# A hybrid decoder trunk on one core: mixer work moved from GpSimd to VectorE, score tiles of one PSUM bank, new spacings in the written order

## The chip, the cores and the metric

One core of a Trainium2 chip runs the whole program, one launch. The metric is the device time of that launch in microseconds (us); less is better. Everything is float32. Matrix products run on TensorE (PE), elementwise work on VectorE (DVE), ScalarE (ACT) and GpSimd (POOL); SyncE (SP) issues the loads of weights. TensorE writes its products to PSUM, 8 banks of 512 float32 per partition, and GpSimd does not touch PSUM anywhere in this program.

## The reference

Two layers, each of three sub-layers on a residual stream x of 512 positions by 1024 features; each sub-layer starts with an RMS norm that is scaled and shifted by values from the vector c, and ends with a gate from c:

```
for l in range(2):
    x += 0.5 * g1 * swiglu_1(mod(norm(x)))          # 1024 -> 2 x 2816 -> 1024
    x += g2 * W_out [ HGRN2 | sparse attention | Mamba-2 ] (mod(norm(x)) @ W_in)
    x += 0.5 * g3 * swiglu_2(mod(norm(x)))
return rms_norm(x)
```

The middle sub-layer, the mixer, holds three independent mixers side by side. HGRN2 (4 heads of 64) is a gated linear recurrence, done in chunks with exact decays. The sparse attention (4 heads of 64, one key and value head) first scores all earlier keys with 8 small index heads, `sum_h w[t,h] relu(q_idx[t,h] . k_idx[s])`, keeps the 128 best for each query, and runs softmax attention over these. Mamba-2 (8 heads of 64, state 128) has a convolution of 4 taps, SiLU, a chunked scan with decays `exp(a_cs[t] - a_cs[s])`, and a gated norm.

## The kernel before, in words

**Products in three parts.** Each float32 operand is split in a high part and the rest (`hi`, `lo`), and each product is three matmuls that accumulate: hi by hi, lo by hi, hi by lo (`mm3`, L342 to L346). A weight is loaded (`wraw`), copied to `whi` on ScalarE (L315), and `wlo = wraw - whi` is made by VectorE, or by GpSimd for the chunks listed in `GF` (L316). There are three buffers of `whi` and `wlo`.

**Feed-forward.** `ffn` runs 22 hidden blocks of 128 and then the product back, in two halves. The next sub-layer's first product starts on the unnormed x while the sum of squares is still on its way; `lead` (L267 on) does that, and folds the shift in by a small product `pb` of a weight that was multiplied with the shift: on GpSimd over 1024 columns (L272), then reduced on VectorE (L276).

**The mixer.** `mixer_woven` holds one dense source and four chains, each a generator that issues instructions and yields how long it wants to wait. `weave` (L327 on) keeps a clock of planned time (`tick`), takes the first whose time has come, and so writes down TensorE's order; TensorE then runs exactly in that order, whatever the real times are. `mark` and `need` tie chains together by planned times; `need_pair` and `hold_pair` book one of two PSUM pairs. The other engines' orders follow the order in which the instructions are traced, their priority, and a list scheduler; `keep_in_program_order` fixes single instructions.

- Dense: the projections (L524, L542 to L544), in the order of `DORD`: forget gates and queries of HGRN2, index keys and queries, attention queries, HGRN2 values, the 8 convolution blocks (`d_conv`: three VectorE steps each at L655, SiLU at L657), then z and g, then the first part of the output projection (`first_out`).
- `topk` scores the index heads (ipl, L706; relu on ScalarE L712, scaled at L719 and summed on GpSimd at L720); `select` takes the 128 best per query in 16 rounds of VectorE's max-of-8 and replace (L732, L735) for each of three blocks.
- `hgrn`: cumulated log decays bf; then seven levels of block sizes 64 down to 1. A level makes differences of bf (L771, L772, VectorE), their exponential (L773, ScalarE), products with k and q (L774, L775, GpSimd), 16 small matmuls into a PSUM pair (lsc, L749), and a predicated copy into the score tile asc (L795). Then four steps over the state (hps, L831 to L863).
- `attends`: scores (apl, L885), maximum and exponential (L895, L898), transposes (apt, L905) and values (apo, L916).
- `ssd`: dt by a series (L933 to L954), cumulated decays (pacs, L957), per block row transposes (prow, L977), decays mt (L1007, L1008), outputs (py) and states (pst).

At the end `project` does the second part of the output projection (po) and adds it to x (L215).

PSUM before: two banks for the dense products (tag mm), two for small ones (sm), and two pairs of two banks (pair). A pair is one tile, and it is free again when its last reader has finished.

Of the kernel before, what the change touches and what calls it, by code (L numbers as in the profile page):

```python
# [18 lines left out]
P = 128  # L19
D = 1024  # L20
S = 512
# [18 lines left out]
LEVLAT = 9.0  # L40
ATTLAT = 10.0
IDXLAT = 3.6
HP = 500
ORD = 'atsh'
DORD = 'hiqvc'
HOLD = 3.5
RES = 4
MTLAT = 8.0
# [6 lines left out]
GF = (6, 7, 8, 9, 10, 11, 12, 13, 14, 15, 16, 17)  # L55
# [9 lines left out]
def body(nc, tc, A):  # L65
    ctx = ExitStack()
    with ctx:
# [199 lines left out]
        def lead(l, i, ws, ps):  # L267
            ts = []
            with tc.high_priority(WAHEAD):
                for wh, wl, raw in ws:  # L270
                    r4 = raw.rearrange("p (a b m) -> p a b m", a=4, b=2)
                    GP.tensor_tensor(r4, r4,  # L272
                                     mod[l][:, i * 6:i * 6 + 4, 1::2][:, :, :, None].to_broadcast([P, 4, 2, P]),
                                     op=OP.mult)
                    r = act("A", "shw", shape=(P, P))
                    V.tensor_reduce(r, raw.rearrange("p (q m) -> p m q", q=NF), axis=AX.X, op=OP.add)  # L276
                    ts.append(r)
# [72 lines left out]
        def begin(pre):  # L350
            with tc.high_priority(0):
# [15 lines left out]
                for step in SEQ:  # L367
# [11 lines left out]
                    else:  # L379
                        j = len(W)  # L380
                        if j < 2:
                            pre[j] = mm("pg"), sm("pu")
                        else:
                            t = pair("pgu")
                            pre[j] = t[:, 0], t[:, 1]
# [108 lines left out]
        def mixer(l, nxt):  # L494
            iqp = pair("pq")
            iqp = [iqp[:, c] for c in range(2)]
# [4 lines left out]
        def mixer_woven(l, nxt, iqp, hh, hl, sb, rb):  # L501
# [123 lines left out]
            def d_index():  # L625
# [5 lines left out]
                mark("ik", 18.0)  # L631
# [14 lines left out]

            def d_conv():
                for f in range(NF):
# [8 lines left out]
                    ACT.activation(t, t, AF.Silu)  # L657
                    xbc.append(t)
                mark("xbc", 6.0)

            def dense():
                hold_pair(16.0)
                for c in DORD:
                    yield from dict(h=d_forget, i=d_index, q=d_query, v=d_value, c=d_conv)[c]()
# [6 lines left out]
                mark("sz", 2.0)  # L671
                sg[:] = [act("C", "sg", shape=(P, 2, 256)) for _ in range(2)]
                yield from tm_group("winG", 256, 4, lambda bp, pp: ACT.activation(sg[bp], pp, AF.Silu))
                mark("sg", 2.0)
                yield from first_out()
# [4 lines left out]
            def topk():  # L680
                yield need("ik")
                for kr in kr_:
                    if kT:
                        yield 3.0
# [11 lines left out]
                for j in range(1, NB):  # L696
# [3 lines left out]
                    for h in range(0, IH, hs):  # L700
# [3 lines left out]
                        for i in range(hs):  # L704
                            ph = slice(i % 2 * 64, i % 2 * 64 + 64)
                            PE.matmul(pl[:, i % 2, i // 2 * n:i // 2 * n + n], iqr[(h + i) // 2][ph, blk(j)],  # L706
# [3 lines left out]
                        for u in range(2):  # L710
                            rl = act("A", "irl")
                            ACT.activation(rl[:, :hs // 2 * n], pl[:, u, :hs // 2 * n], AF.Relu)  # L712
# [31 lines left out]
            def head_pair(name, kx, qx):  # L744
                ps = pair(name)
                for b in range(NB):
                    for u in range(2):
                        ph = slice(u * 64, u * 64 + 64)
                        PE.matmul(ps[:, u, blk(b)], kx[ph, blk(b)], qx[ph, blk(b)], start=True, stop=True)  # L749
# [4 lines left out]
            def hgrn():  # L754
# [11 lines left out]
                def level(m):  # L766
# [6 lines left out]
                    ACT.activation(e, e, AF.Exp)  # L773
                    GP.tensor_tensor(ee[:, :, 0], ee[:, :, 0], v4(k, m)[:, :, 0], op=OP.mult)  # L774
                    GP.tensor_tensor(ee[:, :, 1], ee[:, :, 1], v4(q, m)[:, :, 1], op=OP.mult)  # L775
                    return e

                Asc = [act("B", "asc", shape=(P, 2, S)) for _ in range(2)]
                cur = level(LEVELS[0])
                for f in range(2):  # L780
                    yield need_pair()
                    ps = head_pair("ldg", k[:, f], q[:, f])
                    V.tensor_tensor(b8(Asc[f]), b8(ps), ident[:, None, :].to_broadcast([P, 2 * NB, P]), op=OP.mult)
                ready = clk[0] + 9.0
                for li, m in enumerate(LEVELS):
                    xl = cur
                    for f in range(2):
                        yield need_pair(ready + 2.0 * f)
                        ps = head_pair("lsc", xl[:, f], xl[:, f])
                        if m == 64:  # L790
                            ACT.activation(b8(Asc[f])[:m, :, m:], b8(ps)[:m, :, m:], AF.Copy)
                        else:
                            w = lambda t: t.rearrange("p f (g u m) -> p f g u m", u=2, m=m)[:, :, :, 1]
                            mk = masks[:, li].rearrange("p (g m) -> p g m", m=m)
                            V.copy_predicated(w(Asc[f]), mk[:, None].to_broadcast([P, 2, S // (2 * m), m]), w(ps))  # L795
# [13 lines left out]
                for f in range(2):  # L809
                    for b in range(NB):  # L810
                        PE.transpose(pkd[:, f, blk(b)], k[:, f, blk(b)], ident)
                with tc.high_priority(HP):
                    ACT.activation(kd.rearrange("p f b t -> p (f b t)"), flat(pkd), AF.Copy)
# [9 lines left out]
                for b in range(NB):  # L823
                    yield need_pair(last)
                    last = clk[0] + 7.0
                    hps = pair("hps")
                    po = hps[:, 0, :2 * P].rearrange("p (f c) -> p f c", f=2)
                    vb = vv[b // 2][:, b % 2]
                    if b < NB - 1:
                        for f in range(2):  # L830
                            PE.matmul(hps[:, 1, blk(f)], kd[:, f, b], vb[:, blk(f)], start=True, stop=True)  # L831
# [9 lines left out]
                    hold_pair(4.0)  # L841
                    if b < NB - 1:
                        for f in range(2):
                            pk = hps[:, 1, blk(f)]
                            sn = hst[b % 2][f]
                            for u in range(2):
                                ph = slice(u * 64, u * 64 + 64)
# [406 lines left out]
```

## Time and profile before

| what | value |
|---|---|
| median of 3 runs | 2166.75 us (2165.58 to 2168.28) |
| the profiled execution | 2167.88 us, its span 2166.1 us |
| TensorE matmul busy | 2070.3 us, 96% |
| VectorE busy | 1300.9 us, 60% |
| ScalarE busy | 825.1 us, 38% |
| GpSimd busy | 324.0 us, 15% |
| DMA | 262.5 MB, 121 GB/s on the mean |

The mixer of layer 0 stands at about 415 to 732 us of the span, that of layer 1 at about 1475 to 1792. A share over the span mixes these with feed-forward stretches in which TensorE hardly pauses. The granted clock is a mean of the two levels, 1.2 and 2.4 GHz, as a share of the higher. A row's "waited for" names what released the engine by the profile; for a tile of PSUM that can be the reader that emptied the buffer.

### The profile page before, as it was taken

The numbers are of one execution on the slowest core, as the hardware profiler recorded it, in microseconds if no ns is written. First come the engines' busy times: TensorE is split into PE (matmuls) and PEld (weight loads), VectorE is DVE, ScalarE is ACT, GpSimd is POOL, SyncE is SP. The second block draws the span as 40 slices with busy tenths as digits, with TensorE's granted clock in tenths as the row PEclk, the third lists the DMA queues.
The fourth block names the chain that finished last, engine by engine and source line by source line (L and its number), as shares of the span: only waits on it lengthen the run. The fifth ranks groups of instructions, "written<-read, shape, count | busy, mean of one in ns | idle before, by whom it ended". The sixth has DMA issues, their size and how long they took to land.

```text
span 2166.1 us, 26665 instructions
## 1 busy us (share of the span) xinstructions
PE 2070.3 (96%) x10201; PEld 1711.5 (79%) x10201; DVE 1300.9 (60%) x2338; ACT 825.1 (38%) x1249; POOL 324.0 (15%) x232
## 2 busy tenths in 40 slices
PE   4999999998999999999999999999988999999998
PEld 3888888786787788888878888887767887888886
DVE  7766564688976766433476743357799576333333
ACT  4422223445664432222342222235456644222233
POOL 4000000347401200000010000023662020000001
PEclk9999999999999999999999999999999999999999
DMA  8566562332110356432346753232212123333322
GB/s 304 188 199 235 178 208 85 108 100 57 49 52 30 119 194 237 149 97 86 98 136 214 274 153 97 83 95 91 79 49 59 37 61 98 91 88 113 97 80 77
DMA packets 103536, 262.50 MB, mean 121 GB/s; under 512 B 12272, under 2 KB 14960, under 8 KB 103408
## 3 DMA queue, kind: packets, MB, share of 16 engines
q1 hardware_dynamic: 100016, 256.60, 37.2%
q10 hardware_dynamic: 3392, 4.20, 0.7%
q8 instruction: 80, 1.31, 0.3%
q14 instruction: 48, 0.39, 0.1%
HBM read 255.50 MB, written 2.10 MB: 119 GB/s over the span
## 4 chain that ended last, share of the span: by engine, by line
PE 74%; DVE 14%; ACT 4%; POOL 3%; issue 3%; DMA 2%; ACTq 1%; SPq 0%; POOLq 0%; DVEq 0%
PE pg L344 7%; PE pu L346 7%; PE pg L345 7%; PE pu L344 7%; PE pu L345 7%; PE pg L346 7%; PE pd L345 7%; PE pd L344 7%; PE pd L346 7%; DVE xbc L655 2%; DVE iacc L735 2%; DVE m L732 1%; DVE wlo L316 1%; ACT whi L315 1%; PE po L345 1%
## 5 line engine op out<-in xcount | busy, mean ns | idle before, releaser
L315 ACT ACTIVATE whi<-wraw 128x1024 fp32r<-128x1024 f32 (+1 forms) x374 | 357.2, 957 | 978.0 <-issue 363.4
L316 DVE TENSOR_TENSOR wlo<-wraw,whi 128x1024 fp32r<-128x1024 f32 (+2 forms) x350 | 388.6, 1111 | 371.5 <-ACT whi L315 370.1
L346 PE MATMUL pd<-ahi,wlo 128*128 128x512 f32 (+1 forms) x715 | 275.9, 386 | 0.0
L345 PE MATMUL pd<-alo,whi 128*128 128x512 f32 (+1 forms) x715 | 275.9, 386 | 0.0
L344 PE MATMUL pd<-ahi,whi 128*128 128x512 f32 (+1 forms) x715 | 275.6, 386 | 0.0
L212 POOL TENSOR_TENSOR sq<-sq 128x512 f32<-128x512 f32 x36 | 48.7, 1353 | 1409.3 <-ACT sq L208 1409.1
L346 PE MATMUL pu<-hhi,wlo 128*128 128x512 f32 x656 | 255.7, 390 | 1.6 <-DVE wlo L316 1.6
L344 PE MATMUL pg<-hhi,whi 128*128 128x512 f32 x656 | 255.9, 390 | 0.0
L344 PE MATMUL pu<-hhi,whi 128*128 128x512 f32 x656 | 255.8, 390 | 0.0
L345 PE MATMUL pg<-hlo,whi 128*128 128x512 f32 x656 | 255.7, 390 | 0.0
L345 PE MATMUL pu<-hlo,whi 128*128 128x512 f32 x656 | 255.4, 389 | 0.0
L346 PE MATMUL pg<-hhi,wlo 128*128 128x512 f32 x656 | 255.4, 389 | 0.0
L173 DVE SCALAR_TENSOR_TENSOR adaw<-adaw,crow 128x512 f32<-128x512 f32 x288 | 192.6, 708 | 5.1 <-DMA adaw<-wada 4.7
L440 DVE TENSOR_TENSOR a<-a,pu 128x512 f32<-128x512 f32 x84 | 57.7, 687 | 202.7 <-PE pu L346 202.4
L345 PEld LDWEIGHTS pd<-alo,whi 128*128 128x128 f32 x715 | 134.3, 188 | 27.1
L344 PEld LDWEIGHTS pd<-ahi,whi 128*128 128x128 f32 x715 | 134.3, 188 | 27.1
L346 PEld LDWEIGHTS pd<-ahi,wlo 128*128 128x128 f32 x715 | 134.3, 188 | 26.9
L346 PEld LDWEIGHTS pu<-hhi,wlo 128*128 128x128 f32 x656 | 123.1, 188 | 28.3 <-DVE wlo L316 2.9
L345 PEld LDWEIGHTS pg<-hlo,whi 128*128 128x128 f32 x656 | 123.1, 188 | 26.7 <-DVE hlo L304 1.0
L344 PEld LDWEIGHTS pg<-hhi,whi 128*128 128x128 f32 x656 | 123.1, 188 | 26.6 <-ACT hhi L299 1.3
L344 PEld LDWEIGHTS pu<-hhi,whi 128*128 128x128 f32 x656 | 123.2, 188 | 26.3 <-ACT whi L315 0.8
L345 PEld LDWEIGHTS pu<-hlo,whi 128*128 128x128 f32 x656 | 123.2, 188 | 25.5
(321 smaller groups left out, 3472.0 us busy)
## 6 DMA issues: line engine op xcount, KB each, us to landing
wraw<-wgu SPq DMA_DIRECT2D x176, 512.0 KB, 3.6
adaw<-wada SPq DMA_DIRECT2D x288, 256.0 KB, 5.0
wraw<-wdn SPq DMA_DIRECT2D x64, 384.0 KB, 3.1
wraw<-wdn SPq DMA_DIRECT2D x64, 320.0 KB, 2.9
wraw<-winF SPq DMA_DIRECT2D x36, 512.0 KB, 3.7
wraw<-woutB SPq DMA_DIRECT2D x16, 384.0 KB, 3.0
wraw<-winC SPq DMA_DIRECT2D x8, 512.0 KB, 3.6
rope<-rraw ACTq DMA_DIRECT2D x48, 64.0 KB, 2.6
```

The source lines that it names most:

```text
L173: V.scalar_tensor_tensor(raw, raw, 1.0, crow[:, h], op0=OP.mult, op1=OP.mult, accum_out=part[:, c, h:h + 1])
L212: (eng if f < NF - 1 else V).tensor_add(ssq_t["t"][:, h], ssq_t["t"][:, h], sq[:, h])
L315: ACT.activation(hi, raw, AF.Copy)
L316: (eng or V).tensor_sub(lo, raw, hi.bitcast(F32))
L344: PE.matmul(ps, wh, xh, start=first, stop=False)
L345: PE.matmul(ps, wh, xl, start=False, stop=False)
L346: PE.matmul(ps, wl, xh, start=False, stop=last)
L440: V.tensor_mul(a, a, pu)
L655: V.scalar_tensor_tensor(t[:, s_:], raw[:, :S - s_], cw(3 - s_), t[:, s_:], op0=OP.mult, op1=OP.add)
L732: first = V.max(m8, acc[:, :n])
L735: V.match_replace(acc[:, :n], m8, acc[:, :n], GONE)
```

## The change

- GpSimd's share of the weight splits falls from 12 chunks per mixer to 3 (`GF`); the products of the levels (`LVE`) and, for block 1, the index sums (`IDXV`) go to VectorE; the lead's shift sums become eight VectorE instructions on 128 columns per weight (`LDG`).
- PSUM: no pairs any more. The tag sm has six banks, and `pair` returns two of them. Readers that took a pair in one instruction take each bank by itself (the predicated copies, the diagonal products, kd). The second part of the output projection uses these banks too. The planner still books two pairs.
- The level exponential is traced after the second score product of the level before and is fixed in order; so is the first exponential of each attention group, now after a yield, and the SiLU of each convolution block, one block later.
- Mamba-2's dt series waits for HGRN2's first state (`DTAT`) and has half the steps; half of the decay differences go from ScalarE to VectorE.
- Planned latencies change, the priority of some small instructions is raised, the chains are taken up in another order. The sizes in `SLOTS` and the tile `lev` are as before in the diff.

```diff
-LEVLAT = 9.0
-ATTLAT = 10.0
-IDXLAT = 3.6
+LEVLAT = 6.0
+ATTLAT = 6.5
+IDXLAT = 5.0
-ORD = 'atsh'
-DORD = 'hiqvc'
-HOLD = 3.5
+ORD = 'thas'
+DORD = 'hiqvcCG'
+HOLD = 2.5
+EXLAT = 2.5
+PTLAT = 4.5
+STLAT = 10.0
+DTAT = 'st'
+IDXV = (1,)
+LVE = 'VV'
+LDG = 0
-MTLAT = 8.0
+MTLAT = 12.0
-GF = (6, 7, 8, 9, 10, 11, 12, 13, 14, 15, 16, 17)
+GF = (10, 11, 12)
...
-            return pq.tile(list(shape), F32, name=name, tag="sm", bufs=2)
+            return pq.tile(list(shape), F32, name=name, tag="sm", bufs=6)
         def pair(name):
-            return pq.tile([P, 2, S], F32, name=name, tag="pair", bufs=2)
+            return [sm(name) for _ in range(2)]
...
+                        t = act("A", "shw", shape=(P, P))
+                        V.tensor_scalar(t, raw[:, blk(0)], shift_of(l, i, 0), None, op0=OP.mult)
+                        for q in range(1, NF):
+                            V.scalar_tensor_tensor(t, raw[:, blk(q)], shift_of(l, i, q), t, op0=OP.mult, op1=OP.add)
+                        ts.append(t)
...
+            def silu(f):
+                tc.keep_in_program_order(ACT.activation(xbc[f], xbc[f], AF.Silu))
...
+                                elif j in IDXV:
+                                    V.scalar_tensor_tensor(acc[:, :n], r, w, acc[:, :n], op0=OP.mult, op1=OP.add)
...
-                    ACT.activation(e, e, AF.Exp)
-                    GP.tensor_tensor(ee[:, :, 0], ee[:, :, 0], v4(k, m)[:, :, 0], op=OP.mult)
-                    GP.tensor_tensor(ee[:, :, 1], ee[:, :, 1], v4(q, m)[:, :, 1], op=OP.mult)
                     return e
+                def level_exp(e, m):
+                    ee = v4(e, m)
+                    tc.keep_in_program_order(ACT.activation(e, e, AF.Exp))
+                    g0, g1 = [GP if c == "P" else V for c in LVE]
+                    g0.tensor_tensor(ee[:, :, 0], ee[:, :, 0], v4(k, m)[:, :, 0], op=OP.mult)
+                    g1.tensor_tensor(ee[:, :, 1], ee[:, :, 1], v4(q, m)[:, :, 1], op=OP.mult)
...
-                        if f == 0 and li + 1 < len(LEVELS):
-                            cur = level(LEVELS[li + 1])
-                            nready = clk[0] + LEVLAT
+                        if li + 1 < len(LEVELS):
+                            if f == 0:
+                                cur = level(LEVELS[li + 1])
+                            else:
+                                level_exp(cur, LEVELS[li + 1])
+                                nready = clk[0] + LEVLAT
...
-                    last = clk[0] + 7.0
+                    last = clk[0] + STLAT
...
+                        yield EXLAT + 0.8 * hs
+                            e = ACT.activation(pe, pe, AF.Exp, scale=0.125, bias=mxs[i], accum_out=rsum[:, h:h + 1])
+                            if i == 0:
+                                tc.keep_in_program_order(e)
...
-                yield need("idx1")
+                yield need(DTAT)
...
-                for c in (15, 13, 11, 9, 7, 5, 3, 1):
-                    V.tensor_mul(dt, dt, u3)
-                    V.tensor_scalar(dt, dt, 1.0 / c, None, op0=OP.add)
-                V.tensor_mul(dt, dt, u2)
+                for c in (17, 15, 13, 11, 9, 7, 5, 3):
+                    V.scalar_tensor_tensor(fl(dt), fl(dt), 1.0 / c, fl(u3), op0=OP.add, op1=OP.mult)
+                V.scalar_tensor_tensor(fl(dt), fl(dt), 1.0, fl(u2), op0=OP.add, op1=OP.mult)
...
+                            if g:
+                                V.tensor_scalar(mt[:, r], pr[g][:, blk(r)], acs[:, b, h:h + 1], 0.0,
+                                                op0=OP.subtract, op1=OP.min)
...
-            for _ in project(KO, mm, lambda f: (*weights(A["woutB"][l, f], 768), 0), nxt, True):
+            po = halves("po")
+            for _ in project(KO, lambda _: next(po), lambda f: (*weights(A["woutB"][l, f], 768), 0), nxt, True):
```

## Rows read from the trace of the kernel before

**Rows 1.** The page's part 1: busy us, share of the span, instructions.

```profile
PE 2070.3 (96%) x10201; PEld 1711.5 (79%) x10201; DVE 1300.9 (60%) x2338; ACT 825.1 (38%) x1249; POOL 324.0 (15%) x232
```

**Rows 2.** Windows: busy us (instructions) of PE, PEld, DVE, ACT, POOL; clock; DMA.

```profile
415.00:732.00 317.00, 293.88 (x1818) 245.07 (x1817) 246.59 (x470) 174.91 (x310) 116.79 (x82) 0.95 0.21 60
732.00:1475.00 743.00, 739.78 (x3273) 609.00 (x3271) 402.22 (x689) 231.02 (x301) 34.95 (x22) 1.00 0.46 147
1475.00:1792.00 317.00, 290.35 (x1819) 242.56 (x1819) 249.23 (x470) 173.32 (x310) 116.66 (x83) 0.96 0.21 62
```

**Rows 3.** Windows inside layer 0's mixer.

```profile
500.00:640.00 140.00, 125.48 (x777) 104.28 (x776) 126.26 (x293) 83.50 (x148) 56.93 (x41) 0.91 0.17 50
510.00:520.00 10.00, 5.99 (x25) 4.70 (x24) 9.62 (x16) 0.46 (x1) 6.78 (x5) 0.66 0.19 52
```

**Rows 4.** TensorE's waits, layer 0's mixer: us in total, times, longest.

```profile
PE ipl L706 <- DVE asc L795: 5.9, 2, 4.0
PE lsc L749 <- ACT irl L712: 3.9, 4, 1.5
PE pf L345 <- DVE hlo L304: 3.8, 2, 2.4
PE prow L977 <- ACT dec L965: 3.2, 1, 3.2
PE hps L831 <- ACT yhg L856: 1.5, 1, 1.5
PE po L345 <- DVE yhl L1103: 1.2, 2, 0.9
```

**Rows 5.** TensorE in order of time: start, us, instruction [idle before].

```profile
514.22 1.65 PE L706 MATMUL ipl<-kT,rope 64*128 64x384 f32 x4 [4.01 <-DVE asc L795]
```

**Rows 6.** VectorE in order of time, layer 0, then 746.89 of the next lead.

```profile
508.26 1.45 DVE L946 TENSOR_TENSOR dt<-dt,spw 128x32 f32<-128x32 f32 x1
...
513.47 0.69 DVE L795 COPY_PREDICATED asc<-masks,lsc 128x512 f32<-128x512 uint8 x1
...
516.85 0.19 DVE L946 TENSOR_TENSOR dt<-dt,spw 128x32 f32<-128x32 f32 x1
...
746.89 1.22 DVE L316 TENSOR_TENSOR wlo<-wraw,whi 128x1024 fp32r<-128x1024 f32 x1
```

**Rows 7.** VectorE by line and shape, 415 to 732: busy us, mean ns.

```profile
L316 DVE TENSOR_TENSOR wlo<-wraw,whi 128x1024 fp32r<-128x1024 f32 x16 | 22.1, 1389 | 4.2 <-ACT whi L315 4.2
...
L795 DVE COPY_PREDICATED asc<-masks,lsc 128x512 f32<-128x512 uint8 x12 | 10.9, 910 | 0.4 <-PE lsc L749 0.4
...
L655 DVE SCALAR_TENSOR_TENSOR xbc<-xraw,vec,xbc 128x510 f32<-128x510 f32 x8 | 7.8, 970 | 0.1
...
L946 DVE TENSOR_TENSOR dt<-dt,spw 128x32 f32<-128x32 f32 x8 | 5.6, 702 | 0.2
...
L771 DVE TENSOR_TENSOR lev<-bf 128x512 f32<-128x512 f32 x7 | 4.8, 681 | 0.0
```

**Rows 8.** VectorE by line and shape, 498 to 600.

```profile
L947 DVE TENSOR_SCALAR dt<-dt 128x32 f32<-128x32 f32 x8 | 5.4, 680 | 0.2
...
L863 DVE TENSOR_TENSOR yhg<-yhg,hss 128x256 f32<-128x256 f32 x4 | 1.7, 420 | 0.2 <-POOL hss L861 0.2
...
L895 DVE CUSTOM_DVE_ANT_0 pexp<-apl,cst 128x128 f32<-128x128 f32 x4 | 0.9, 282 | 0.0
```

**Rows 9.** GpSimd by line and shape, 415 to 732.

```profile
L316 POOL TENSOR_TENSOR wlo<-wraw,whi 128x1024 fp32r<-128x1024 f32 x11 | 27.0, 2456 | 33.3 <-ACT whi L315 33.3
L775 POOL TENSOR_TENSOR lev<-lev,hq 128x512 f32<-128x512 f32 x7 | 11.5, 1637 | 0.0
...
L774 POOL TENSOR_TENSOR lev<-lev,kf 128x512 f32<-128x512 f32 x7 | 10.4, 1483 | 2.1 <-ACT lev L773 2.1
...
L720 POOL TENSOR_TENSOR iacc<-iacc,irl 128x256 f32<-128x256 f32 x7 | 5.8, 833 | 0.4
```

**Rows 10.** ScalarE by line and shape, 415 to 732: idle before.

```profile
L773 ACT ACTIVATE lev<-lev 128x1024 f32<-128x1024 f32 x7 | 7.4, 1058 | 7.4 <-DVE lev L772 5.8 <-DVE lnv L579 1.5
```

More of the change, by code (lines that the diff above doesn't have):

```diff
@@ L268, in lead @@
             ts = []
[L269 to L277, printed above, removed]
+            if LDG:
+                with tc.high_priority(WAHEAD):
+                    for wh, wl, raw in ws:
+                        r4 = raw.rearrange("p (a b m) -> p a b m", a=4, b=2)
+                        GP.tensor_tensor(r4, r4,
+                                         mod[l][:, i * 6:i * 6 + 4, 1::2][:, :, :, None].to_broadcast([P, 4, 2, P]),
+                                         op=OP.mult)
+                        r = act("A", "shw", shape=(P, P))
+                        V.tensor_reduce(r, raw.rearrange("p (q m) -> p m q", q=NF), axis=AX.X, op=OP.add)
+                        ts.append(r)
+            else:
+                with tc.high_priority(WAHEAD):
+                    for wh, wl, raw in ws:
+                        t = act("A", "shw", shape=(P, P))
[3 more added lines that the diff above has]
+                        ts.append(t)
             pb = sm("pb", (P, 2))
@@ L656, in d_conv, with d_z @@
                                                op0=OP.mult, op1=OP.add)
-                    ACT.activation(t, t, AF.Silu)
                     xbc.append(t)
[L659 to L664, printed above, removed]
+                    if f:
+                        silu(f - 1)
+                yield
+                yield
+                yield
+                silu(NF - 1)
+                mark("xbc", 3.0)
+            def d_z():
                 sz[:] = [act("C", "sz") for _ in range(NB)]
@@ L674, in dense @@
                 mark("sg", 2.0)
+            def dense():
+                hold_pair(16.0)
+                for c in DORD:
+                    yield from dict(h=d_forget, i=d_index, q=d_query, v=d_value, c=d_conv, C=d_z, G=d_g)[c]()
                 yield from first_out()
@@ L748, in head_pair @@
                         ph = slice(u * 64, u * 64 + 64)
-                        PE.matmul(ps[:, u, blk(b)], kx[ph, blk(b)], qx[ph, blk(b)], start=True, stop=True)
+                        PE.matmul(ps[u][:, blk(b)], kx[ph, blk(b)], qx[ph, blk(b)], start=True, stop=True)
                 tick(1.15)
@@ L782, in hgrn @@
                     ps = head_pair("ldg", k[:, f], q[:, f])
-                    V.tensor_tensor(b8(Asc[f]), b8(ps), ident[:, None, :].to_broadcast([P, 2 * NB, P]), op=OP.mult)
-                ready = clk[0] + 9.0
+                    for par in range(2):
+                        V.tensor_tensor(b3(Asc[f][:, par]), b3(ps[par]), ident[:, None, :].to_broadcast([P, NB, P]),
+                                        op=OP.mult)
+                level_exp(cur, LEVELS[0])
+                ready = clk[0] + 6.0
                 for li, m in enumerate(LEVELS):
@@ L810, in hgrn @@
                     for b in range(NB):
-                        PE.transpose(pkd[:, f, blk(b)], k[:, f, blk(b)], ident)
+                        PE.transpose(pkd[f][:, blk(b)], k[:, f, blk(b)], ident)
                 with tc.high_priority(HP):
-                    ACT.activation(kd.rearrange("p f b t -> p (f b t)"), flat(pkd), AF.Copy)
+                    for f in range(2):
+                        ACT.activation(kd[:, f], b3(pkd[f]), AF.Copy)
                 mark("kd", 0.0)
@@ L830, in hgrn @@
                         for f in range(2):
-                            PE.matmul(hps[:, 1, blk(f)], kd[:, f, b], vb[:, blk(f)], start=True, stop=True)
+                            PE.matmul(hps[1][:, blk(f)], kd[:, f, b], vb[:, blk(f)], start=True, stop=True)
                     for f in range(2):
@@ L963, in ssd @@
                 dec = sp.tile([P, 3, NB, SH], F32, name="dec", bufs=1)
-                V.tensor_copy(fl(acs), pa[:, 0])
-                ACT.activation(dec.rearrange("p i b h -> p i (b h)"), pa, AF.Exp)
+                with tc.high_priority(HP):
+                    V.tensor_copy(fl(acs), pa[:, 0])
+                    ACT.activation(dec.rearrange("p i b h -> p i (b h)"), pa, AF.Exp)
                 dsd = act("A", "dsd", shape=(P, 4, P))
@@ L969, in ssd @@
                 sss = sp.tile([P, NB, 2], F32, name="sss")
+                yield 3.0
                 def decays(b):
@@ L1013, in outputs @@
                     yield need_pair(ready)
-                    pp = pair("py")
-                    py, pf = pp[:, 0], pp[:, 1]
+                    py = sm("pyd")
                     for f in range(4):
@@ L1104, in ysplit, with halves @@
                     yh[f], yl[f] = hi, lo
+            def halves(name):
+                t = []
+                while True:
+                    if not t:
+                        pp = pair(name)
+                        t = list(pp)
+                    yield t.pop(0)
             def project(ks, tile, load, nxt, last):
@@ L1118, in first_out @@
             def first_out():
-                yield need("hgrn")
+                yield need("hgrn", "sg")
                 for i in range(2):
```

104 lines of the change are left out of this document (58 added, 46 removed).

## The prediction

> **What bounds the kernel now.** I read the page's busy shares first, then the stretches of the span, then TensorE's waits inside the slow stretches, then what VectorE and GpSimd do while TensorE waits. TensorE's row has 2070.3 of 2166.1 us [rows 1], so VectorE's 60% and GpSimd's 15% say nothing until one looks stage by stage. The feed-forward stretch between the two mixers has TensorE busy 739.78 of 743 us at a granted clock of 1.00: nothing to win there. The two mixers, 317 us each, are where time goes lost: 293.88 and 290.35 us busy, and clocks of 0.95 and 0.96 [rows 2]. That is 23.1 + 26.7 us without a matmul, and 0.05 x 317 + 0.04 x 317 = 15.9 + 12.7 us given away to the lower clock level: 39.0 and 39.4 us, 78 us in all. This is the whole purse of the change.
>
> In layer 0 most of it lies in 140 us, from 500 to 640: TensorE busy 125.48 (14.5 us idle), clock 0.91 (12.6 us), together 27.1 of the 39.0; and there VectorE is busy 126.26 of the 140, in one slice 9.62 of 10 [rows 3]. So in that stretch TensorE waits for a VectorE that is nearly full. Which waits these are: index scores for a VectorE copy into asc (5.9 us), level scores for a ScalarE relu (3.9), the row transposes for the decays (3.2), state products for a ScalarE copy (1.5); and, at its start, the first projections for the lead's low halves (3.8) [rows 4]. Neither of the first two is a wait for data: an index score does not read asc. They are waits for a PSUM pair to come free. The longest shows the chain: TensorE stood 4.01 us before the index product at 514.22 [rows 5], until a predicated copy that began at 513.47 and took 0.69 us had emptied the pair; that copy stood behind dt's small steps, 32 elements wide, which took 1.45 us each there and 0.19 us some microseconds later [rows 6], and after this idle the slice 510 to 520 has a granted clock of 0.66, so a good part of it at 1.2 GHz in place of 2.4.
>
> **The change part by part, for one layer.** VectorE's load decides, so I sum that first.
>
> It adds on VectorE: nine of the twelve weight splits that GpSimd did, 9 x 1.22 us = 11.0 (1.22 undisturbed [rows 6]; 1.39 on the mean [rows 7], which makes 12.5); the level products, 14 x 0.68 = 9.5, by another 512-wide operation of two SBUF inputs [rows 7]; the index sums of block 1, 7 x 0.42 = 2.9 by a 256-wide product; the decay differences of the second group, 16 x 0.28 = 4.5 by the 128-wide operation from PSUM [rows 8] (no such instruction is in the trace: 0.19 for 32 elements and 0.42 for 256 bound it, 3.0 to 6.7); the predicated copies in halves, 24 x 0.42 - 12 x 0.69 = 1.8 [rows 6, 8]. Sum 29.7.
>
> It takes from VectorE: dt's 8 + 8 polynomial steps, 5.6 + 5.4 us [rows 7, 8], become 9 of 0.19 = 1.7 [rows 6], so -9.3. And the time that VectorE loses beside GpSimd: a convolution step takes 0.97 us where 0.68 is the undisturbed width, 24 of them, 7.0 us; predicated copies 12 x (0.91 - 0.69) = 2.6; splits 16 x 0.17 = 2.7 [rows 6, 7]: 12.3 together. GpSimd itself loses 9 x 2.46 + 11.5 + 10.4 + 5.8 = 49.8 of its 116.8 us [rows 2, 9], a bit under half. Bounds of what comes back are 0 and 12.3; I take 8, as most convolution steps ran beside the very splits that leave. Net per layer 29.7 - 9.3 - 8 = +12.4 us on VectorE, 259 of 317: it fits on the whole.
>
> In the tight 140 us the account is another: of the additions there fall five splits (6.1), two of seven levels (2.7), four of seven index sums (1.7), seven of the twelve predicated copies (1.0) and half the decay differences (2.2), 13.7; of the removals all of dt (9.3) and about 7 of the 8: -16.3. VectorE's work there goes from 126.3 to 123.7 us. The fullest slice shown has it at 0.96 [rows 3]; filled to 0.97, a hundredth more, the stretch would be 127.5 us. So of the 27.1 us that TensorE loses there, VectorE lets at most 140 - 127.5 = 12.5 us go.
>
> Does the change remove that much of the waits? Single-bank tiles turn two pairs into six banks: a third pair is there, and a bank is released by its own reader. With that go the waits for a pair, 5.9 + 3.9 us, and the clock they cost. Moving dt behind the first state removes the stall at 513; it is next needed by the cumulative sums, which wait for the last convolution, late in the stretch, so it is hidden. The 3.2 us of the row transposes go, since VectorE's copy is put first and the plan yields 3 us before them; the state products (1.5) get 10 us of spacing for 7. That is 14.5 us of waits and up to 12.6 us of clock: more than VectorE's 12.5, so VectorE is what is late next, and 12.5 is the term. The lead's 3.8 us stays: the two splits that GpSimd did in its midst become 2 x 1.22 us on the same VectorE queue as the low halves.
>
> At nothing I cost: the lead's shift sums (16 narrow VectorE instructions for two GpSimd products and two reductions; TensorE does not wait for shw in rows 4; uncovered, 16 x 0.28 = 4.5 us for each of five leads); the output projection in six banks in place of two (its rows show waits for its operands, not for a bank); ScalarE's loss of seven scalings and 16 relus (it is no bound: idle parts cover it, and it loses work). No transfer is added, removed or moved past a queue. Of the headline, the buffer counts of the SBUF classes and the level tile are the same in the diff, and the top-k step was already held in order, so nothing is summed for these.
>
> Outside the 140 us the plan's own latencies work against it. An attention group of four heads gets 2.5 + 3.2 + 6.5 + 2 + 4.5 = 18.7 us where it had 10 + 2 + 3.5 = 15.5, a group of two 16.1 for 14.5. As long as projections are left to weave in, that costs nothing; the last two groups come when they have run out, 2 x 1.6 = 3.2 us. Against it stand some 3.3 us of clock outside the stretch (15.9 - 12.6), part of which goes with shorter waits. I set this to zero.
>
> Sum: 2 layers x 12.5 = 25 us. The profiled execution took 2167.88 us (span 2166.1), which gives 2142.9; it lies 1.1 us over the median of the runs, 2166.75, and so the forecast for the median is 2142 us.
>
> **The rivals.** (1) VectorE is no bound: with the plan nearer to what runs, the top-k steps slide into the holes of 640 to 732. For it: after 640 there is VectorE time to spare (246.59 - 126.26 = 120.3 us in 177 [rows 2, 3]). Against: top-k runs held in order. Then all 27.1 us of the stretch go in both layers: 2166.75 - 54 = 2112.
>
> (2) Banks were only where the wait showed. Then the third pair buys nothing, the PSUM waits turn into waits for the same VectorE instructions as data, and only the dt stall goes: 4.0 us and its clock, 0.34 x 10 = 3.4, less the 3.2 us of the longer attention tail and 3 us of level products queued on VectorE: 2 x 1.2 us, 2164, no change that can be told. For it: VectorE's 0.96 in that slice. Against: the relu that the level scores wait for has no use for them. The Trainium skill has a rule on this side, in "TensorE: Matmul & The Clock Gate", section "HAM oscillation — how this bites in real kernels": in a kernel already kept dense, "Adding PSUM double-buffering gave no further gain". By that rule the sum would be this rival's; rows 4 do show waits that only a free bank ends, which that kernel need not have had.
>
> (3) Slower: the order pinned on ScalarE. Seven level exponentials, eight silus and six first attention exponentials, 21 per layer, now stand in program order in front of the weight copies (whi) on ScalarE's queue. Before, ScalarE was idle 7.4 us ahead of the seven level exponentials, 1.06 us each, mostly for lev from VectorE [rows 10]. If the plan is early, that idle time is ScalarE's with a weight copy behind it, and TensorE runs out of weights. It decides from 12.5 / 21 = 0.6 us of TensorE time for each; at the 1.06 us of these rows it costs 22 us per layer, net +9.8, so 2166.75 + 20 = 2186. For it: VectorE, on which each exponential waits, is full there. Against: three weight buffers stand ahead.
>
> **How the numbers follow.** Forecast (10 to 40 us faster) 0.56; rival 1 0.17; rival 2 0.13, of which I count 0.05 as just faster; rival 3 0.14. A change of 0.2%, 4.3 us, is about what a measurement of this kernel can tell from none. Faster 0.56 + 0.17 + 0.05 = 0.78, the same 0.07, slower 0.01 + 0.14 = 0.15. For 8 in 10 the range goes from rival 1's 2112, a little under it, 2110, to 2168, where rival 2 ends with no gain from dt; what lies out is a tenth above and some below.
>
> **What would show it.** Right: in both mixers no wait of ipl or lsc for another tile's reader over 1 us, dt steps of 0.2 us, GpSimd some 65 us per mixer, TensorE idle in the mixers down by 12 to 18 us per layer and a mixer clock of 0.97 or more, VectorE still over 0.9 in the middle of the mixer. Rival 1: VectorE falls below 0.9 there. Rival 2: the waits keep their sum and name VectorE data. Rival 3: new waits of pf, pt or po for whi or wlo. Wrong altogether if the feed-forward stretches move, or if the two layers go different ways.

## The result and the profile after

The changed kernel takes 2113.28 us (median of 4 runs, 2112.45 to 2113.57), the kernel before 2167.52 (2165.58 to 2169.29): a ratio of 0.9749, interval 0.9732 to 0.9766, or 54 us off. The forecast was 2142, a gain of 25: the direction held and the range held the time, but the gain is more than twice the one forecast. The first row is part 1 of the changed kernel's page (to set against [rows 1]):

```profile
PE 2049.5 (97%) x10201; PEld 1697.5 (80%) x10201; DVE 1298.7 (62%) x2510; ACT 818.5 (39%) x1213; POOL 213.6 (10%) x162
```

TensorE's busy time falls by 20.8 us with the same 10201 matmuls, which goes with the clock (mean granted clock 0.992 for 0.984); the other 33.6 us of the span's 54.4 are idle time of TensorE. VectorE, which received GpSimd's work, is busy 2.2 us less over the span, not more. Windows of the changed kernel, columns as in [rows 2]: both mixers, from the first to the next lead's shift product, then the old tight stretch, then what follows the last dense product of layer 0:

```profile
415.00:719.00 304.00, 295.28 (x1880) 246.62 (x1878) 256.19 (x546) 176.12 (x299) 73.65 (x53) 0.99 0.23 68
1444.00:1748.00 304.00, 295.43 (x1875) 246.90 (x1874) 255.02 (x545) 175.55 (x299) 74.17 (x53) 0.98 0.22 68
500.00:640.00 140.00, 134.04 (x899) 113.67 (x897) 130.51 (x323) 99.82 (x176) 43.48 (x33) 0.99 0.19 56
628.00:719.00 91.00, 87.56 (x493) 73.57 (x491) 70.03 (x128) 45.97 (x86) 15.57 (x14) 1.00 0.20 60
```

The same mixers in the kernel before (the row of layer 1 starts 2.4 us late, its first shift product stands at 1472.61), and the last 91 us of layer 0's, after its last dense product:

```profile
415.00:746.00 331.00, 306.65 (x1880) 255.32 (x1878) 257.50 (x482) 179.90 (x317) 120.16 (x84) 0.95 0.21 62
...
1475.00:1803.00 328.00, 300.11 (x1866) 250.37 (x1866) 257.14 (x479) 176.57 (x314) 118.16 (x84) 0.96 0.22 63
...
655.00:746.00 91.00, 85.91 (x461) 70.95 (x459) 63.16 (x92) 41.97 (x82) 20.82 (x17) 0.98 0.20 63
```

From shift product to shift product the mixers lose 27.0 and 25.8 us, the feed-forward between them 1.7. In layer 0 VectorE does 256.2 us of work where it did 257.5, and its idle time falls from 73.5 to 47.8 us. TensorE's waits in layer 0's mixer, changed kernel (against [rows 4]):

```profile
PE pt L557 <- ACT xraw L670: 3.1, 1, 3.1
PE apt L957 <- ACT mt L1064: 2.3, 1, 2.3
PE pf L361 <- DVE hlo L320: 1.9, 2, 1.5
PE po L360 <- DVE x L222: 0.3, 1, 0.3
```

The waits for a pair (ipl, lsc), of the row transposes for the decays (prow) and of the state products (hps) are gone; none of them is in the list of layer 1 either. VectorE by line and shape in the changed mixer, 415 to 719 (against [rows 7]):

```profile
L332 DVE TENSOR_TENSOR wlo<-wraw,whi 128x1024 fp32r<-128x1024 f32 x25 | 30.4, 1215 | 4.3 <-ACT whi L331 4.3
...
L831 DVE COPY_PREDICATED asc<-masks,lsc 128x256 f32<-128x256 uint8 x24 | 11.4, 539 | 0.7 <-PE lsc L778 0.7
...
L673 DVE SCALAR_TENSOR_TENSOR xbc<-xraw,vec,xbc 128x510 f32<-128x510 f32 x8 | 6.0, 749 | 0.1
...
L746 DVE SCALAR_TENSOR_TENSOR iacc<-irl,kv,iacc 128x256 f32<-128x256 f32 x7 | 5.4, 771 | 0.3
...
L808 DVE TENSOR_TENSOR lev<-lev,kf 128x512 f32<-128x512 f32 x7 | 5.0, 715 | 0.0
```

The additions cost what was summed, or more (index sums 0.77 for 0.42 each); the neighbours became cheaper: the 0.97 of a convolution step is 0.75 here, 0.785 on the mean of all 24, where the prediction's sum went down to 0.68.

### The profile page after: what moved, and what is told of

It is laid out like the page before. It is cut to its first block, busy times and chain, and to the rows that moved or that the text cites. A ratio compares the mean times of both kernels' runs of the same rounds, so it can differ in the third digit from the quotient of the medians.

```text
span 2111.7 us, 26662 instructions
## 1 busy us (share of the span) xinstructions
PE 2049.5 (97%) x10201; PEld 1697.5 (80%) x10201; DVE 1298.7 (62%) x2510; ACT 818.5 (39%) x1213; POOL 213.6 (10%) x162
## 4 chain that ended last, share of the span: by engine, by line
PE 87%; DVE 7%; ACT 4%; issue 1%; DMA 1%; POOL 0%; SPq 0%; DVEq 0%; ACTq 0%; POOLq 0%
PE pd L360 8%; PE pd L361 8%; PE pd L362 8%; PE pg L361 7%; PE pu L362 7%; PE pu L361 7%; PE pg L362 7%; PE pg L360 7%; PE pu L360 7%; PE pf L360 2%; PE pf L361 2%; PE pt L557 2%; PE pf L362 2%; PE pt L558 1%; PE pt L559 1%; PE lsc L778 1%
## 5 line engine op out<-in xcount | busy, mean ns | idle before, releaser
L332 DVE TENSOR_TENSOR wlo<-wraw,whi 128x1024 fp32r<-128x1024 f32 (+3 forms) x368 | 401.8, 1092 | 369.3 <-ACT whi L331 367.7
L360 PEld LDWEIGHTS pd<-ahi,whi 128*128 128x128 f32 x715 | 134.3, 188 | 27.1
```

The lines of the kernel that those rows point to most:

```text
L332: (eng or V).tensor_sub(lo, raw, hi.bitcast(F32))
L360: PE.matmul(ps, wh, xh, start=first, stop=False)
```

## The experiments

Microseconds off before are (1 - ratio) x 2167.5, each against the kernel before on the same chip. On this scale the change is 54.4. The intervals of the ratios are 0.001 to 0.003 to each side, 2 to 6 us.

**Undoing one part of the changed kernel.** Two pairs and two single banks in place of six banks:

```diff
-            return [sm(name) for _ in range(2)]
+            t = pq.tile([P, 2, S], F32, name=name, tag="pair", bufs=2)
+            return [t[:, 0], t[:, 1]]
```

> The changed kernel with PSUM as before: two pairs of two banks, each one tile, and two single banks; all else as changed. Theory B with the banks as its main part: the waits for a pair come back, 9.8 us and their clock per layer, about 2150 us. Rival (the banks did little once GpSimd's work and dt were out of the way): within 6 us of the changed kernel, 2119 or less.

Ratio 0.9886 [0.9866, 0.9906], 24.7 off, near the 2150 of theory B: the banks are worth 29.7 within the change. All of GpSimd's work back (the decay differences, which came from ScalarE, stay on VectorE):

```diff
-IDXV = (1,)
-LVE = 'VV'
-LDG = 0
-GF = (10, 11, 12)
+IDXV = ()
+LVE = 'PP'
+LDG = 1
+GF = (6, 7, 8, 9, 10, 11, 12, 13, 14, 15, 16, 17)
```

> The changed kernel with GpSimd's work put back: all twelve splits, level products, index sums of block 1 and the lead's shift sums. Theory A: VectorE's queue has about 12 us less per mixer of its own work, but loses up to 12 beside GpSimd, so the time stays within 8 us, 2105 to 2121. Theory C (the gain is the loss beside GpSimd and the long GpSimd steps in the level chain): half of the gain or more goes, 2140 us or more. Theory B with banks as its main part: 2115 to 2130.

Ratio 0.9874 [0.9853, 0.9894], 27.3 off, at the edge of theory C: the moved work is worth 27.1. Part 1 of its page, with VectorE at 1298.2 beside the changed kernel's 1298.7 above:

```profile
PE 2057.1 (96%) x10201; PEld 1700.5 (80%) x10201; DVE 1298.2 (61%) x2380; ACT 829.9 (39%) x1231; POOL 328.3 (15%) x232
```

So 114.7 us of GpSimd's busy time went to VectorE and VectorE's busy time did not move: what it took on, it got back from its other instructions. Old distances and order of the plan:

```diff
-LEVLAT = 6.0
-ORD = 'thas'
-HOLD = 2.5
+LEVLAT = 9.0
+ORD = 'atsh'
+HOLD = 3.5
...
```

(and the index, state, decay and attention distances as before). Two things are not as before: an attention group keeps its extra yield of 0.8 us per head, and a level's 9 us count from the second score product of the level before, where the kernel before counts them from the first.

> The changed kernel with the planned latencies and the order of the chains as before (level 9, attention 10 without the extra yield, index 3.6, hold 3.5, state 7, decays 8). If the banks and VectorE's share make the gain and the plan's figures only fit themselves to it: 2113 to 2122. If the figures carry a good part of it: 2130 or more.

Ratio 0.9838 [0.982, 0.9856], 35.1 off: undoing these numbers costs 19.3; how much of it comes from the longer way of counting a level's 9 us, no run shows. The pins on ScalarE (the instructions that are fixed in program order) taken out:

```diff
-                tc.keep_in_program_order(ACT.activation(xbc[f], xbc[f], AF.Silu))
+                ACT.activation(xbc[f], xbc[f], AF.Silu)
```

(and the same for the two exponentials).

> The changed kernel without the three pins (level exponential, SiLU, first attention exponential). In the changed trace a pinned attention exponential keeps ScalarE idle for 7.07 us and TensorE waits 3.1 us behind it, once per layer. If pins only cost: 6 us less, 2107. If they keep exponentials and SiLUs from changing places, and so the order near what the planner assumes: slower, 2120 us or more, with more table loads than the changed kernel.

Ratio 0.9734 [0.9714, 0.9754]: no difference to the change. Rival 3 falls.

**One part alone on the kernel before.** Six banks; dt's edit (its place and the steps halved); the moved work; the plan's numbers, each as in the diff of the change (of the plan, a level's 6 us count from the first score product here, so it is a tighter plan than that of the changed kernel, and attention's longer distances stand in one yield):

```diff
-            return pq.tile([P, 2, S], F32, name=name, tag="pair", bufs=2)
+            return [sm(name) for _ in range(2)]
```

> The kernel before with one part of the change: single-bank tiles (six banks, each reader takes its bank); GpSimd's work, dt, latencies and pins as before. Theory B (waits for a pair): the 5.9 + 3.9 us of pair waits and part of their clock go in each layer, 2140 to 2150. Theory A (VectorE's work bounds the mixer before as after, so the waits only change their name): 2160 or more.

```diff
-                yield need("idx1")
+                yield need("st")
```

> The kernel before with dt alone changed: begun after the first state in place of the first index block, half of the steps. By the prediction's term 4.0 us of wait and 3.4 us of clock per layer: 2153 us. If the copy that emptied the pair is then held up by the next thing on VectorE: 2162 to 2167.

```diff
-                    GP.tensor_tensor(ee[:, :, 0], ee[:, :, 0], v4(k, m)[:, :, 0], op=OP.mult)
+                    V.tensor_tensor(ee[:, :, 0], ee[:, :, 0], v4(k, m)[:, :, 0], op=OP.mult)
```

> The kernel before, with only the moved GpSimd work of the change (nine weight splits, the level products, the index sums of block 1, the lead's shift sums on VectorE, and the second group's decay differences from ScalarE to VectorE), with the pairs, dt's place and the plan's numbers as before. Theory A (parts add up; undoing this work in the changed kernel cost 29 us): about 2140. Theory B (parts pay only together): within 12 us of before, as the banks alone and dt alone did, 2155 to 2170; by the prediction's own account VectorE gains 12.4 - 9.3 for dt's missing part, that is about 22 us per layer of load with nothing taken away, which at 0.8 would be slower, 2185 to 2200.

```diff
-LEVLAT = 9.0
-ORD = 'atsh'
-HOLD = 3.5
+LEVLAT = 6.0
+ORD = 'thas'
+HOLD = 2.5
...
```

> The kernel before, with the plan's numbers and the order of the changed kernel only (levels at 6 for 9, index 5 for 3.6, state 10 for 7, decays 12 for 8, attention's distances longer, hold 2.5 for 3.5, the order of the four threads); the products of the levels stay on GpSimd. Theory A (distances and order gain by themselves): 2147, the 20 us that undoing them costs in the changed kernel. Theory B (they pay only where the operands come as early as they say): no gain or slower, 2165 to 2180.

Banks 0.9942 [0.9927, 0.9957], 12.6 off; dt 0.9939 [0.9918, 0.9961], 13.2 off; the moved work 0.9999 [0.999, 1.0009], nothing; the plan alone 1.0157 [1.0141, 1.0172], 34 us slower. The banks lie between their two theories, dt gives what the prediction's term says, 2153, within 3 us. In the last two theory B held, beyond its range for the plan. With the moved work alone VectorE is busy 1323.6 us, 22.7 more than before, and the time is the same; the prediction's VectorE account would have made it slower. With the plan alone TensorE's waits in layer 0's mixer are led by this row, in place of the 3.9 us of lsc in [rows 4]:

```profile
PE lsc L749 <- DVE asc L795: 14.0, 5, 7.9
```

A plan that asks for the level scores 6 us after the first score product before them, where GpSimd still makes the products and two pairs hold the scores, writes down an order that TensorE then has to wait for. Banks and dt together:

```diff
+            return [sm(name) for _ in range(2)]
...
+                yield need("st")
```

> The kernel before, with the six single banks and dt's steps moved and halved, nothing else. Theory A (the two waits are separate, parts add): 2167.4 - 11 - 12 = 2144. Theory B (a stall that one removes returns as the other's): one gain only, 2155. Theory C (both needed for the top-k steps to start early): more than the sum, 2135 or less.

Ratio 0.9836 [0.982, 0.9853], 35.5 off, where 12.6 and 13.2 add up to 25.8: theory C. The rows, out of the lists of TensorE's waits in layer 0's mixer, show how one stall stands behind the other. First the banks alone: the index product waits for no pair, and the next in order, a level score, stands in its place. The row names dt, which a level score does not read; the score begins at 517.06, after a predicated copy out of PSUM that ran from 516.49 to 516.91, behind dt steps of up to 2.27 us. Then dt alone, with the pair waits still there:

```profile
PE lsc L748 <- DVE dt L950: 4.3, 1, 4.3
```

```profile
PE lsc L749 <- ACT irl L712: 3.3, 3, 2.2
PE ipl L706 <- DVE asc L795: 2.6, 1, 2.6
```

With both, lsc is not in the list and ipl has 0.3 us; the longest wait is one that VectorE's update of the state ends. That row, and 500 to 640:

```profile
PE hps L837 <- DVE hst L856: 4.0, 1, 4.0
```

```profile
500.00:640.00 140.00, 133.57 (x902) 113.06 (x902) 121.65 (x306) 94.58 (x174) 59.19 (x43) 0.98 0.17 51
```

**VectorE's load priced.** Ballast is work whose result nobody uses. Two additional maxima of 512 elements per convolution block, 16 x 0.69 = 11 us per layer, 22 in all:

```diff
                     xbc.append(t)
+                    for _ in range(2):
+                        mx8 = sp.tile([P, 8], F32, name="mx8")
+                        V.max(mx8, raw)
```

On the changed kernel:

> The changed kernel with two more max-of-8 on VectorE (512 wide, 0.69 us, nobody reads the result) after each convolution block: 16 x 0.69 = 11.0 us per mixer, no part of the top-k chain. The ballast on the top-k rounds gave back 23 of 27 us. If VectorE's load bounds the changed mixer: about +20 again, 2133. If it was the length of the top-k chain that told there: at most +8, 2121 or less.

on the kernel before:

> The kernel before, with two additional maxima of 512 elements per convolution block on VectorE (8 blocks, 16 instructions, about 11.0 us per layer by their 0.69 us each in the same experiment on the changed kernel, where the 22 us of both layers cost 17.4). Their results are not used. Theory A (VectorE bounds the kernel before in the stretch as well, as the prediction took it): 0.8 us per us again, +17 us, about 2185. Theory B (before, the pairs, dt's place and the plan's distances hold TensorE, and VectorE has 73 us of idle time in a mixer, some of it where a convolution step can go): the price is under half of that, +8 us or less, at most 2176.

on before with banks and dt:

> The kernel before with the six banks and dt's edit (2130.3 us), and the same ballast in the convolution as before, 11 us of VectorE per layer, 22 in all, results unused. Theory A (VectorE becomes the bound as soon as the waits for a bank and for dt are gone): 0.8 us per us, about 2148. Theory B (GpSimd's late products and the plan's longer distances hold it there, and VectorE has slack): under 6 us, 2130 to 2136.

On the changed kernel 0.9825 [0.9809, 0.984], 16.5 us dearer: 0.75 us per us. On the kernel before 0.9985 [0.9973, 0.9997], no cost at all. On before with banks and dt 0.9922 [0.9896, 0.9948], 18.6 dearer: 0.85 per us. The prices are per us of ballast; VectorE's busy time rises by less, by 20.2, 13.0 and 16.1 us. So VectorE's load in the convolution did not bound the kernel before, for all its 126 of 140 us; it has a price as soon as the waits for a bank and for dt are gone. With banks and dt most of that price is one wait in each layer, of the cumulated decays for dt's result, which stands late on the loaded VectorE:

```profile
PE pacs L965 <- DVE da L960: 6.6, 1, 6.6
```

In the loaded kernel before, the same stretch has VectorE at 131.74 and TensorE no less busy than in [rows 3], and the old stall stands, in order of time, 3 us later. The convolution and its ballast begin only at 540, so they don't make that shift, and the price is that of load behind the stall, not ahead of it:

```profile
500.00:640.00 140.00, 126.39 (x799) 104.80 (x798) 131.74 (x308) 86.30 (x152) 58.23 (x43) 0.94 0.17 50
```

```profile
517.36 1.65 PE L709 MATMUL ipl<-kT,rope 64*128 64x384 f32 x4 [4.04 <-DVE asc L798]
```

A second ballast in the changed kernel, one more maximum per two top-k rounds (13.4 us per layer), sits in the chain of top-k:

```diff
                         if r % 2 == 1:
+                            mx8 = sp.tile([P, 8], F32, name="mx8")
+                            V.max(mx8, acc[:, :n])
```

> The changed kernel with one more max-of-8 on VectorE, whose result nobody reads, after every second top-k round: 8 x (0.43 + 0.56 + 0.69) = 13.4 us more VectorE work per mixer, most of it in the middle of the mixer. Theory A, of the prediction (VectorE's work in the middle of the mixer bounds its length): each us added comes back, +13 per layer, about 2140 us. Theory B (TensorE waited for the order of the instructions and for buffers, and VectorE's work slides into room elsewhere): at most 4 per layer, 2121 us or less.

Ratio 0.9848 [0.9824, 0.9871], 21.5 dearer for 26.8: 0.80 per us, a price in a chain that the intervals don't tell from that beside one. The other direction, two of three convolution steps left out (taps at distances 2 and 3 are missing):

```diff
-                    for s_ in range(1, 4):
+                    for s_ in range(1, 2):
```

> The changed kernel, with two of the convolution's three steps left out on VectorE (part of the computation is missing: the taps at distances 2 and 3), 16 x 0.785 = 12.6 us per layer, 25 us in all. Theory A (VectorE is still the bound at 0.8 us per us): up to what TensorE still loses in the mixers, 8.7 us idle and about 3 us of clock per layer, less the 3.8 us at the lead: -12 to -16 us, 2098 to 2101. Theory B (the price is one-sided: the plan's order and TensorE's own work are the floor now, and only additional work is late): -5 us or less, 2108 to 2113.

Ratio 0.971 [0.9695, 0.9724], 8.5 us better for 25 us less: 0.34 per us, between the two theories. TensorE has 8.6 us idle per mixer left to win, which may be the reason; no run shows it.

**Which of the moved work counts.** Nine splits back on GpSimd (`GF` as before), or the level products back (`LVE = 'PP'`):

```diff
-GF = (10, 11, 12)
+GF = (6, 7, 8, 9, 10, 11, 12, 13, 14, 15, 16, 17)
```

> The changed kernel with nine weight splits per layer back on GpSimd, the level products, index sums and shift sums staying on VectorE. By undisturbed times VectorE is relieved of 9 x 1.215 = 10.9 us per layer and GpSimd gets 9 x 2.4 = 21.6. Theory A (the splits carry the cost, by late weights and by what VectorE loses beside them): most of the 29 us, 2130 to 2142. Theory B (the level products carry it): 2113 to 2120. If VectorE's load were all, it would be faster, 2113 - 17 = 2096.

```diff
-LVE = 'VV'
+LVE = 'PP'
```

> The changed kernel with the 14 level products per layer back on GpSimd, everything else as changed. VectorE is relieved of 9.8 us per layer. Theory A (the splits carry the cost): 2105 to 2118. Theory B (a level product on GpSimd makes the level scores late by the shorter distance of 6 in the plan, and the queue behind them): 2125 to 2142.

Splits 0.9802 [0.9787, 0.9816], 11.5 dearer; products 0.983 [0.9812, 0.9847], 17.6 dearer; together 29.1, where all the moved work was 27.1. Both carry it: for the products theory B held, for the splits the time lies between the two. With 18 splits taken off it in the two layers (21.9 us), VectorE is busy 1300.7 us in all, no less than the 1298.7 with them; with the 28 level products taken off it, 1305.5.

**A better version.** The copy of the convolution's input put ahead on ScalarE, no pins; then also the second group's decays back on ScalarE:

```diff
-                    ACT.activation(raw, ps, AF.Copy)
+                    with tc.high_priority(HP):
+                        ACT.activation(raw, ps, AF.Copy)
```

> The changed kernel without its three pins, and with the copy of the convolution's input out of PSUM (xraw) put ahead on ScalarE's queue, where TensorE waited 3.1 us once per layer. If that wait is a cost of its own: 2113 - 1.4 - 6.2 = 2106. If another instruction is late in its place: 2110 to 2113.

```diff
-                            if g:
+                            if g > 1:
```

> The changed kernel without pins, xraw's copy ahead (2110.9 us), and the second group's decay differences on ScalarE as in the kernel before: 16 instructions, 4.5 us per layer off VectorE, some more on ScalarE, which is busy 176 of 304 us. Theory A (VectorE's load is the price, 0.4 to 0.8 us per us both ways): 2 x 4.5 x 0.4 to 0.8 less, 2104 to 2107. Theory B (ScalarE's decays are late instead, TensorE already waits 2.3 us for them in the changed kernel): 2111 to 2118.

The first: 0.9738 [0.9721, 0.9754], 2110.91 us, not told apart from the change, as the second case expected; among its waits, pt's for xraw only fell from 3.1 to 2.0 and pf now waits for the same copy, 2.6. The second: 0.9775 [0.9747, 0.9803], 8 us worse than the first, theory B's time and a little more. Its reason is not shown: TensorE waits 0.2 us for decays in layer 0, and its new wait is for VectorE's yss (pyt, 2.8). No version here is told apart from the change as a better one.

## Why the prediction was right and wrong

**What bounded the kernel before: half right.** The pair waits and the dt stall were read rightly, the clause that TensorE waits "for a VectorE that is nearly full" was not: 22 us of ballast in the convolution cost nothing, and the moved work alone, with 22.7 us more on VectorE, left the time as it was. The 0.96 of the slice was a chain of small steps that happened to stand in front of the release.

**The step that failed** is the term "VectorE lets at most 12.5 us go" per layer; 27.0 and 25.8 went. That VectorE is what is late next is right (0.75 to 0.85 us per us). The term, 140 - 123.7 / 0.97, is not: it takes VectorE's work in the stretch, shuts it in and fills the stretch to 0.97, and it was wrong at two places.

First, the load. For the layer the prediction has +12.4 us; measured it is -1.3 (256.19 for 257.50). The busy times of all groups in layer 0's mixer, added up, go from 276.9 to 281.5 us (groups overlap, so the sums exceed the engine's busy time): additions of some 36 us (splits 10.9, level products 9.8, index sums 5.4, decay differences 4.5, shift sums 4.3, copies 0.8) and dt's -9.3 would make about +26, so some 20 us came back from other instructions, where I took 8 and gave 12.3 as the upper end. I had looked for it only in convolution steps, predicated copies and splits; it lay in the rotary sums too (1.22 to 0.69 us each), in ht (2.1 us in all), hlo, xlo, and the small steps of kv (about 1 us off each of four). The +12.4 is not in the forecast's sum, but seven eighths of the 8 are. An estimate of what that weighs: with seven eighths of 20 in the stretch, and its additions scaled up like those of the layer, from 13.7 to 16.6, the term is 140 - 116.1 / 0.97 = 20.3. The Trainium skill states in "SBUF — State Buffer", section "Who interferes with whom", that VectorE and GpSimd share a port pair as an exclusive lock, and that a VectorE instruction with two SBUF inputs contends with a GpSimd instruction that reads SBUF. The two traces agree: the rotary sums, which got cheaper, have two such inputs, and top-k's maxima over 512 elements, with one, take 0.69 us in both. By it the relief would have been looked for in every instruction of two SBUF inputs beside GpSimd.

Second, the floor: I shut VectorE's work into the 140 us and filled them to 0.97. It isn't shut in, and TensorE's products did not end with it. Top-k's maxima, before and after (first and last start):

```profile
L732 DVE MAX8 m<-iacc x48: 413/557/695, 521.0 to 631.7; 128x8 f32<-128x256 f32 x16, 128x8 f32<-128x384 f32 x16, 128x8 f32<-128x512 f32 x16
...
L761 DVE MAX8 m<-iacc x48: 392/553/696, 505.4 to 627.7; 128x8 f32<-128x256 f32 x16, 128x8 f32<-128x384 f32 x16, 128x8 f32<-128x512 f32 x16
```

Top-k begins 16 us earlier but ends only 3 to 4 us earlier, while the last dense product ends at 628 where it ended at 655: TensorE's products, which ended 22 us behind top-k, caught up with it (in layer 1 top-k ends 1.4 us earlier after the first shift product, the last dense product 25). Up to the last dense product VectorE's idle time falls from 45.7 to 26.8 us, and 6.9 us more of its work lie behind it, 70.03 of the last 91 us for 63.16: with the 1.3 us less work these are the 27 us of layer 0. How the miss divides between the load and the floor, no run shows.

**The removals: right in kind, wrong as a sum.** Waits for ipl and lsc gone, dt steps at 0.209 us, both as named. But I added a pair wait and a dt wait as two terms; alone they give 12.6 and 13.2, with both in place 35.5. In the rows above the other stall stands in its place when one goes.

**What I set at zero.** Undoing the plan's distances costs 19.3 us within the change, and a tighter plan cost 34 without it; the rest of the change, moved work and plan above all, gives 54.4 - 35.5 = 18.9 over banks and dt, and with either one of the two undone nothing is left of it (35.1 and 27.3 off). The lead's 3.8 us did not stay: it is 1.9, and 1.9 too where the moved work is the only change.

**The rivals.** Rival 1 has the right number, 2112, and part of the reason: VectorE's work did slide behind the dense products. That VectorE is no bound is not what the runs show: it stays at 0.93 of 500 to 640, and its load has a price. Rival 2: banks alone gave 12.6 us, banks with dt 35.5, and undoing them costs 29.7, so the runs decide against it; a part of it is true, banks alone turned one wait into another, that of lsc behind dt's steps. The "no further gain" that the Trainium skill reports of another kernel, in "TensorE: Matmul & The Clock Gate", section "HAM oscillation — how this bites in real kernels", does not hold for this one. Rival 3's mechanism shows once per layer, the 3.1 us of pt, and its price is none.

**The signs.** TensorE's idle time fell by 15.6 us in layer 0 (24.35 to 8.72), within the 12 to 18, and by 19.3 in layer 1 (27.9 to 8.6), just over; the clock is 0.99 and 0.98; GpSimd 74 us per mixer for some 65; VectorE is over 0.9 in the middle; the feed-forward stretch moved by 1.7 of 727 us; both layers went alike.

## What to carry to other kernels

A full engine is a bound only if load on it costs time: put ballast on it in the kernel as it is (here 22 us cost nothing), and again where the suspected waits are taken out (here 0.85 us per us). Such a price holds for the place where the ballast stands, so see in the waits what it makes late. Waits that stand one behind the other in a written order are not terms of a sum: taking away one shows the next, and the gain comes with the last. A distance in a plan that is shorter than its operand needs is paid as a wait (14.0 us of lsc here): change the producer first, then the distance.

## What the runs showed of the hardware

Moving GpSimd's work (328.3 to 213.6 us busy) to VectorE left VectorE's busy time where it was (1298.2 and 1298.7 us): beside GpSimd, VectorE lost in this kernel as much as the moved work costs it. A VectorE instruction can end with the GpSimd instruction beside it: in the kernel before, dt's step of 508.26 [rows 6] ended at 509.71, GpSimd's product of 508.14 at 509.66. Narrow instructions lose most for their length: dt's 32-element steps went from 0.69 us on the mean to 0.209 [rows 7], and with GpSimd's work back and dt at its new place they took 0.428.
